# Delta net's values and keys turned by VectorE, second operands by operand for four output tiles, merges a step later

## The chip, the cores and the metric

The kernel runs on 1 core of one Trainium2 chip, in one launch. The metric is the device time of that core in microseconds (us), the median of three runs. The core has a matrix engine (PE), a vector engine (DVE), a scalar engine (ACT), GpSimd (POOL) and SyncE (SP), which here only issues DMAs; each works through its own instruction list in order and waits on semaphores.

## The reference

Two layers on a sequence of 1024 tokens and 1024 channels: layer 0 is a mixer of retention and a gated delta net, layer 1 a gated linear recurrence (RG-LRU); a feed-forward part with a causal convolution stands behind each, and every part begins with an RMS norm. The parts that the change touches are the delta net and the two output products `y @ w_out` and `(gelu(gate) * hs) @ lru_w_out`:

```python
qkv = jax.nn.silu(causal_dwconv(jnp.concatenate([q_d, k_d, v_d], axis=-1), conv_w))
...
lmat = jnp.where(strict, jnp.einsum('bhnid,bhnjd->bhnij', k_beta, kc) * decay, 0.0)
rhs = jnp.concatenate([vc * bc, k_beta * jnp.exp(gc)[..., None]], axis=-1)
sol = lax.linalg.triangular_solve(lmat + jnp.eye(c, dtype=jnp.float32), rhs,
                                  left_side=True, lower=True)
...
def step(s, inp):
    u_n, w_n, a_n, qd_n, kt_n, cd_n = inp
    v_new = u_n - jnp.einsum('bhcd,bhdv->bhcv', w_n, s)
    o = jnp.einsum('bhcd,bhdv->bhcv', qd_n, s) + jnp.einsum('bhij,bhjv->bhiv', a_n, v_new)
    s = s * cd_n + jnp.einsum('bhcd,bhcv->bhdv', kt_n, v_new)
    return s, o
...
y = jnp.concatenate([y_r, y_d.reshape(b, t, GDN_WIDTH)], axis=-1).astype(hn.dtype)
return y @ w_out
```

Four heads of 128 channels; the state is carried from chunk to chunk. Everything is float32.

## The kernel before

Activations lie in SBUF with channels on partitions and tokens along the row, in two halves of 512 tokens. A float32 product is made of three matmuls of rounded parts: `mm3` (L313 to L315) adds high times high, high times low and low times high. One such product of a 128x128 piece of a weight with 512 tokens is what the text calls a product, or a slot. P224, say, is the place in PE's list where 224 of them have run.

Weights arrive as "quarters" of 128x512 in an order fixed by a table. The SP queue loads one into a `raw` buffer (L257), ACT makes the rounded high part `whi` (L267), DVE subtracts to the low part `wlo` (L268). They are numbered from the kernel's start; six are held ready. Weights 44 and 45 are those of gate 14, weights 46 and 47 those of retention's q of head 0, 48 and 49 those of its k.

The order of each engine's list is set when the kernel is built, by a scheduler that takes the instructions as the program issues them and weighs when their operands come. The program issues side work in lanes, one step every two slots. In the delta net the lane runs, one after another: `subst`, a forward substitution of all 32x32 blocks on DVE (L1332, L1334), which stores the inverses to DRAM in two forms, `t_dram[0]` and `t_dram[1]` (L1337, L1339), then idles 11 steps; and a `merge` for each of four heads, which loads those blocks back, one form through SP and the other through POOL (L1353), and joins them to 128x128 inverses by small matmuls: L1369, L1378 and L1382, L1392, L1398 on PE, with copies between these on ACT (L1363, L1364, L1372, L1385, L1386, L1394, L1399) and L1400 on DVE. Beside this, the main stream projects units of 128 channels: q's heads, gates 12 and 13 (L1167 tanh on ACT, L1168 on DVE, stored to `g_dram`), v's heads, gate 14, then retention's q and k. A v head is evicted by L373, goes through its convolution (L1264 on ACT, L1266 three times on DVE) and an activation (L1268, L1269), and is stored to `v_dram` by one DMA of 512 KB (L1721). The rotary tables come by two DMAs that ACT issues (L1736 for the second) and are multiplied by the norm's row on DVE (L1737, L1738); retention's q and k are evicted with them (L1538, L1540, L1541).

The scan then runs over 8 chunks of 128 tokens. `scan_load` fetches v and q of a chunk (L1446, L1447). `scan_inside` turns v's four heads on PE with the identity (L1461) and scales the result out of PSUM on DVE (L1462), multiplies keys by queries (L1465), and turns K's four heads of the chunk (L1473, L1474) except in the last chunk. `scan_state` (L1485, L1491, L1498, L1508, L1509) carries the state.

`part` makes the two output products: for a group of output tiles m and each half u of the operands, it takes one quarter of tile m and multiplies it by its four operands in turn; in u == 1 the sum is added to the residual (L533). Groups are the first four output tiles of a half together, and then single tiles. The operands' rounded parts are made by L586 (ACT) and L587 (DVE).

Of the kernel before, what the change touches and what calls it, by code (L numbers as in the profile page):

```python
# [13 lines left out]
F32 = mybir.dt.float32  # L14
F32R = mybir.dt.float32r
AF = mybir.ActivationFunctionType
ALU = mybir.AluOpType
AX = mybir.AxisListType

P = 128  # L20
# [3 lines left out]
HALF = 512  # L24
NCH = T // P
NH = 4
# [72 lines left out]
def bc_last(ap, n):  # L99

    return ap.unsqueeze(2).to_broadcast([ap.shape[0], ap.shape[1], n])


class Block:
# [405 lines left out]
    def part(self, ys, name, groups, sl, each, kept=None):  # L510


        w = sl.stop - sl.start
        n, c0 = divmod(sl.start, HALF)
        for ms in groups:
            ps = {m: self.pp(both=True)[:, 0:w] for m in ms}
            for u in range(2):
                for m in ms:
                    if kept is None:
                        hi, lo = self.quarter((name + "ab"[u], m))  # L520
                    else:
                        if (u, m) not in kept:
                            kept[u, m] = self.load_kept(self.I[name + "ab"[u]][m], 4 * m + 2 * u)
                        hi, lo = kept[u, m]
                    nk = min(4, len(ys) - 4 * u)
                    for kt in range(nk):
                        c = slice(kt * P, (kt + 1) * P)
                        yh, yl = (a[:, c0:c0 + w] for a in ys[4 * u + kt][n])
                        self.mm3(ps[m], hi[:, c], lo[:, c], yh, yl, u == 0 and kt == 0, u == 1 and kt == nk - 1)
                        self.slot()  # L530
                    if u == 1:
                        h = self.H[m][:, sl]
                        self.nc.vector.tensor_tensor(h, ps[m], h, ALU.add)  # L533
                        each(m, h)
# [609 lines left out]
    def mix0(self, gain):  # L1144
        tc = self.tc
        self.q_dram = tc.dram_tile([NCH, P, HALF], F32, name="q_dram")
        self.ry_dram = tc.dram_tile([4, NCH, P, P], F32, name="ry_dram")
        self.v_dram = tc.dram_tile([NCH, P, HALF], F32, name="v_dram")
        self.gc_dram = tc.dram_tile([NH, NCH, P], F32, name="gc_dram")
        self.l_dram = tc.dram_tile([P, 32, 32], F32, name="l_dram")  # L1150
        self.t_dram = tc.dram_tile([2, P, 32, 32], F32, name="t_dram")
        self.y_dram = tc.dram_tile([8, P, T], F32, name="y_dram")
        self.rv_dram = tc.dram_tile([NCH, P, HALF], F32, name="rv_dram")
        self.g_dram = tc.dram_tile([NH, P, T], F32, name="g_dram")
        self.X = [[(self.slots1(4 * k + n), self.slots1(4 * k + 2 + n)) for n in range(2)] for k in range(KT)]
        with tc.tile_pool(name="l0", bufs=1) as pool:
            gd = self._mix0(pool.tile([P, 24 * HALF], F32, name="l0"))
        self.s2_stack = ExitStack()
        self.open_s2(self.s2_stack)
        self._mix0_out(gain, gd)  # L1160
# [10 lines left out]
    def _mix0(self, room):  # L1171
        tc, nc, I = self.tc, self.nc, self.I
        V, A, G, PE = nc.vector, nc.scalar, nc.gpsimd, nc.tensor
        H = self.H
        ps4 = lambda ps: ps.rearrange("p (h c) -> p h c", h=4)
        hs = lambda h: slice(h * P, (h + 1) * P)
# [83 lines left out]
        def conv_tail(kind, h, buf, dst):  # L1260
            ti = {"q": 0, "k": 4, "v": 8}[kind] + h
            c = self.t()
            w = lambda j: self.col("gdn_conv", 4 * ti + j)
            A.activation(c, buf[:, 1:1 + T], AF.Copy, scale=w(0))  # L1264
            for j in (1, 2, 3):
                V.scalar_tensor_tensor(c, buf[:, 1 + j:1 + j + T], w(j), c, ALU.mult, ALU.add)  # L1266
            th = self.t() if dst is None else dst
            A.activation(th, c, AF.Tanh, scale=0.5)  # L1268
            V.scalar_tensor_tensor(th, th, 1.0, c, ALU.add, ALU.mult)  # L1269
            return th  # L1270

        def conv_head(kind, h, dst):
            unit = conv_unit(kind, h)
# [169 lines left out]
        def scan_load(n):  # L1443
            t = chunk[n]
            t.update({"q": tmp2("qc"), "v": spare["v"][n % 2], "e": spare["e"][n % 2], "kt": spare["kt"][n % 2]})
            nc.sync.dma_start(t["v"], self.v_dram[n])  # L1446
            nc.sync.dma_start(t["q"], self.q_dram[n])  # L1447

        def scan_inside(n):
            cs = slice(n * P, (n + 1) * P)  # L1450
            cn = lambda t: hn(t)[:, :, n]
            q, v, gr, e, kt = (chunk[n][i] for i in ("q", "v", "gr", "e", "kt"))
            V.tensor_tensor(ps4(e), ps4(gr), bc_mid(sq["m_attn"], 4), ALU.add)
            for h in range(NH):
                A.activation(e[:, hs(h)], e[:, hs(h)], AF.Exp, bias=col(ngcc, h, n))
            for h in range(NH if n else 0):
                A.activation(gr[:, hs(h)], gr[:, hs(h)], AF.Exp, bias=col(cen, h, n))
            yield
            pv = self.pc()
            for h in range(NH):  # L1460
                PE.transpose(pv[:, hs(h)], v[:, hs(h)], self.ident)  # L1461
            V.tensor_tensor(ps4(v), ps4(pv), bc_last(cn(cv), P), ALU.mult)  # L1462
            p = self.pc()
            for h in range(NH):
                PE.matmul(p[:, hs(h)], K[h][:, cs], q[:, hs(h)], start=True, stop=True)  # L1465
            V.tensor_tensor(e, e, p, ALU.mult)
            if n:
                V.tensor_tensor(q, q, gr, ALU.mult)
            yield
            if n < NCH - 1:  # L1470
                p = self.pc()
                for h in range(NH):
                    PE.transpose(p[:, hs(h)], K[h][:, cs], self.ident)  # L1473
                V.tensor_tensor(ps4(kt), ps4(p), bc_last(cn(ekt), P), ALU.mult)  # L1474
            yield

        def scan_state(n):
# [213 lines left out]
        def subst():  # L1691
            yield from range(3)
            sub = subst_load()
            yield from range(2)
            for j in range(31):
                subst_step(*sub, j)
                yield
            subst_store(*sub)
            yield from range(11)
        gdn += [subst()]  # L1700
        for h in range(NH):
            gdn += [together(merge(h, 0), merge(h, 1))]
        for h in range(NH):
# [6 lines left out]
            if h % 2:  # L1710
                values(h // 2)

        def gates2(heads):
            for h in heads:
                g = self.gate2(self.unit("mix_in", 12 + h))
                nc.sync.dma_start(self.g_dram[h], g)
        scan_row(0)
        gates2((0, 1))
        for h in range(NH):
            v = conv_head("v", h, None)  # L1720
            nc.sync.dma_start(self.v_dram[:, :, hs(h)].rearrange("n p c -> p n c"),  # L1721
                              v.rearrange("p (n c) -> p n c", n=NCH))
        gates2((2,))
        self.flush()
        S = [tmp2("S0"), tmp2("S1")]
# [142 lines left out]
```

## Time and profile before

| | |
|---|---|
| median of 3 runs | 2149.26 us (2147.45 to 2149.64) |
| the profiled execution | 2149.09 us |
| its span, first to last instruction | 2147.3 us |
| mean granted clock of PE | 0.999 |
| moved by DMA | 307.98 MB, 143 GB/s over the span |

The profile's rows give line, engine, operation, output and input, with the count, and then busy time in us, mean in ns, and the idle time before with the instruction that ended it. Rows of a timeline begin with the start and the duration in us. Stretches of the delta net in the profiled execution: `subst` stores at 168.8 and 170.0 us, merges from 179.3 to 249, the scan's first chunk from 262.9, mix_out (layer 0's output product) around 490.

### The profile page before, as it was taken

Reading aid. Unit: us, or ns where it says so; the run is one execution under the profiler, and the core shown is the slowest. Engines: PE = TensorE matmul, PEld = TensorE weight load, DVE = VectorE, ACT = ScalarE, POOL = GpSimd, SP = SyncE. Lnnn points to the kernel's source line nnn. Section 1 sums busy time; section 2 is a strip of 40 time slices with the busy share of each in tenths; the row PEclk is TensorE's granted clock in tenths of the full one; section 3 lists DMA queues with packets and bytes.
Section 4 is the critical chain, followed back from the end, with each engine's and each line's share of the span. In section 5 each row is a group of like instructions: output and inputs, shape, how many; then the busy total and the mean of one; then the engine's idle time right before and its main releaser. Section 6 shows DMA issues by size and latency. Waiting matters only on the chain.

```text
span 2147.3 us, 29614 instructions
## 1 busy us (share of the span) xinstructions
PE 2131.8 (99%) x10652; PEld 1776.5 (83%) x10652; DVE 1704.7 (79%) x2581; ACT 1074.1 (50%) x1732; POOL 96.8 (5%) x114
## 2 busy tenths in 40 slices
PE   9999999999999999999999999999999999999998
PEld 7877888887888888888888888888888888888887
DVE  7995677766999989888766786778999889888645
ACT  6444522234665555555324476755655555554221
POOL 0102022200000000000000000000000000000001
PEclk9999999999999999999999999999999999999999
DMA  5354433543145435438725312252354445375542
GB/s 187 93 168 126 136 94 88 173 146 114 50 163 178 152 141 191 157 113 275 240 99 198 89 50 82 68 157 64 123 181 167 146 154 176 118 267 183 176 169 84
DMA packets 237171, 307.98 MB, mean 143 GB/s; under 512 B 62912, under 2 KB 125920, under 8 KB 237024
## 3 DMA queue, kind: packets, MB, share of 16 engines
q1 hardware_dynamic: 201344, 299.60, 41.8%
q10 hardware_dynamic: 34656, 5.97, 1.5%
q8 instruction: 84, 1.38, 0.3%
q0 software_dynamic: 1024, 0.53, 0.1%
q14 instruction: 63, 0.52, 0.1%
HBM read 215.27 MB, written 90.74 MB: 143 GB/s over the span
## 4 chain that ended last, share of the span: by engine, by line
PE 64%; issue 30%; DVE 3%; DMA 2%; POOL 0%; ACT 0%; SPq 0%; POOLq 0%; DVEq 0%; ACTq 0%
PE ps L313 19%; PE ps L315 19%; PE ps L314 19%; PE pc L313 1%; PE pc L314 1%; PE pc L315 1%; DVE h L973 0%; DVE l L1332 0%; DVE l L1334 0%; PE pc L1491 0%; PE pc L1577 0%; PE pc L1465 0%; PE ps L1509 0%; PE ps L1607 0%; DVE h L1303 0%
## 5 line engine op out<-in xcount | busy, mean ns | idle before, releaser
L313 PE MATMUL ps<-s,whi 128*128 128x512 f32 (+1 forms) x2704 | 1053.6, 390 | 2.5 <-ACT s L586 1.4
L314 PE MATMUL ps<-s,whi 128*128 128x512 f32 (+1 forms) x2704 | 1048.2, 388 | 1.2 <-DVE s L587 0.7
L315 PE MATMUL ps<-s,wlo 128*128 128x512 f32 (+1 forms) x2704 | 1047.5, 388 | 0.0
L267 ACT CAST whi<-raw 128x512 fp32r<-128x512 f32 (+1 forms) x620 | 377.0, 613 | 634.5 <-PE ps L314 499.7
L313 PEld LDWEIGHTS ps<-s,whi 128*128 128x128 f32 x2704 | 507.8, 188 | 108.2 <-ACT s L586 2.3
L314 PEld LDWEIGHTS ps<-s,whi 128*128 128x128 f32 x2704 | 508.0, 188 | 104.5 <-DVE s L900 1.8
L315 PEld LDWEIGHTS ps<-s,wlo 128*128 128x128 f32 x2704 | 507.7, 188 | 104.4 <-DVE wlo L268 0.6
L268 DVE TENSOR_TENSOR wlo<-raw,whi 128x512 fp32r<-128x512 f32 (+1 forms) x620 | 418.0, 680 | 64.0 <-ACT whi L267 55.2
L828 DVE SCALAR_TENSOR_TENSOR t<-halo,cols,t 128x1024 f32<-128x1024 f32 x176 | 221.7, 1281 | 2.1 <-ACT t L826 1.0
L801 DVE TENSOR_TENSOR halo<-ps,kept 128x512 f32<-128x512 f32 (+1 forms) x138 | 92.0, 667 | 76.4 <-PE ps L315 75.6
L811 DVE TENSOR_TENSOR h<-ps,h 128x512 f32<-128x512 f32 x112 | 77.3, 690 | 79.1 <-PE ps L315 79.1
L826 ACT ACTIVATE t<-halo,cols 128x1024 f32<-128x1024 f32 x88 | 109.6, 1247 | 18.0 <-DVE halo L801 9.9
L796 ACT COPY kept<-ps 128x512 f32<-128x512 f32 (+1 forms) x138 | 77.0, 558 | 11.0 <-PE ps L315 9.5
L533 DVE TENSOR_TENSOR h<-ps,h 128x512 f32<-128x512 f32 (+1 forms) x72 | 45.2, 630 | 42.0 <-PE ps L315 41.8
L916 DVE TENSOR_TENSOR t<-t 128x1024 f32<-128x1024 f32 x44 | 53.7, 1221 | 0.0
L911 ACT ACTIVATE t<-t 128x1024 f32<-128x1024 f32 x44 | 46.8, 1063 | 10.0 <-DVE t L828 10.0
L852 ACT CAST t<-t 128x512 fp32r<-128x512 f32 x56 | 34.0, 622 | 34.7 <-DVE t L916 32.7
L401 ACT ACTIVATE t<-h 128x512 f32<-128x512 f32 (+1 forms) x49 | 27.3, 563 | 44.2 <-DVE h L533 44.2
L313 PE MATMUL ps<-s,s 128*128 128x256 f32 (+1 forms) x144 | 46.0, 320 | 0.0
L314 PE MATMUL ps<-s,s 128*128 128x256 f32 (+1 forms) x144 | 45.8, 318 | 0.0
L315 PE MATMUL ps<-s,s 128*128 128x256 f32 (+1 forms) x144 | 45.8, 318 | 0.0
L1266 DVE SCALAR_TENSOR_TENSOR t<-halo,cols,t 128x1024 f32<-128x1024 f32 x33 | 41.9, 1278 | 2.9 <-ACT t L1264 2.6
(337 smaller groups left out, 2113.3 us busy)
## 6 DMA issues: line engine op xcount, KB each, us to landing
raw<-in_ffn_up_dram SPq DMA_DIRECT2D x176, 256.0 KB, 2.7
s<-pf_dram SPq DMA_DIRECT2D x112, 256.0 KB, 5.1
sf_dram<-t SPq DMA_DIRECT2D x72, 256.0 KB, 2.5
raw<-in_ffn_w_dram SPq DMA_DIRECT2D x64, 256.0 KB, 3.0
t<-sf_dram SPq DMA_DIRECT2D x58, 256.0 KB, 4.2
pf_dram<-t SPq DMA_DIRECT2D x56, 256.0 KB, 2.6
pf_dram<-lo SPq DMA_DIRECT2D x56, 256.0 KB, 2.6
raw<-in_mix_in_dram SPq DMA_DIRECT2D x52, 256.0 KB, 3.0
```

Source lines behind the costliest of these rows:

```text
L267: self.nc.scalar.copy(hi[:, 0:w], raw[:, 0:w])
L268: eng.tensor_tensor(lo[:, 0:w], raw[:, 0:w], f32(hi[:, 0:w]), ALU.subtract)
L313: mm(ps, whi, xhi, start=start, stop=False)
L314: mm(ps, whi, xlo, start=False, stop=False)
L315: mm(ps, wlo, xhi, start=False, stop=stop)
L796: A.copy(kept[o], ps)
L801: V.tensor_tensor(dst(i, j), v(ps), v(kept[k]), ALU.add)
L811: V.tensor_tensor(h(*to[o]), ps.rearrange("p (h c) -> p h c", c=256), h(*to[o]), ALU.add)
L826: A.activation(t, buf[:, 2:2 + T], AF.Identity, scale=w(0), bias=self.col(f"ffn_cb{layer}", tile_i))
L828: V.scalar_tensor_tensor(t, buf[:, 2 + j:2 + j + T], w(j), t, ALU.mult, ALU.add)
L911: A.activation(tg, tg, AF.Silu)
L916: V.tensor_tensor(tg, tg, tv, ALU.mult)
```

## The change

Three edits. In `part`, the second half of the operands of a group of four tiles takes its four quarters together and runs over the operands outside and the four tiles inside. In the delta net, DVE transposes each v head and each K head in blocks of 32x32 (one instruction for 128x1024), and four DMAs each, one for every 32 partitions, write the blocks turned to DRAM, in pieces of 32 numbers; a chunk's v and k are then loaded in the orientation that the scan needs, and PE's transposes go. `free[0]` is the buffer of the convolution that has become free; `slots(14 + ...)` are buffers that `subst` used. `subst` idles 12 steps instead of 11.

```diff
@@ part @@
             for u in range(2):
+                if u == 1 and len(ms) > 1:
+                    hold = self.qpos
+                    ws = [self.quarter((name + "b", m), 0, hold) for m in ms]
+                    for kt in range(len(ys) - 4):
+                        c = slice(kt * P, (kt + 1) * P)
+                        yh, yl = (a[:, c0:c0 + w] for a in ys[4 + kt][n])
+                        for m, (hi, lo) in zip(ms, ws):
+                            self.mm3(ps[m], hi[:, c], lo[:, c], yh, yl, False, kt == len(ys) - 5)
+                            self.slot()
+                    for m in ms:
+                        h = self.H[m][:, sl]
+                        self.nc.vector.tensor_tensor(h, ps[m], h, ALU.add)
+                        each(m, h)
+                    continue
...
@@ conv_head @@
             V.scalar_tensor_tensor(th, th, 1.0, c, ALU.add, ALU.mult)
+            free[0] = c
             return th
+
+        free = [None]
...
@@ scan_load @@
             nc.sync.dma_start(t["q"], self.q_dram[n])
+            if n < NCH - 1:
+                nc.sync.dma_start(t["kt"], self.k_dram[n])
...
@@ scan_inside @@
-            pv = self.pc()
-            for h in range(NH):
-                PE.transpose(pv[:, hs(h)], v[:, hs(h)], self.ident)
-            V.tensor_tensor(ps4(v), ps4(pv), bc_last(cn(cv), P), ALU.mult)
+            V.tensor_tensor(ps4(v), ps4(v), bc_last(cn(cv), P), ALU.mult)
...
-                p = self.pc()
-                for h in range(NH):
-                    PE.transpose(p[:, hs(h)], K[h][:, cs], self.ident)
-                V.tensor_tensor(ps4(kt), ps4(p), bc_last(cn(ekt), P), ALU.mult)
+                V.tensor_tensor(ps4(kt), ps4(kt), bc_last(cn(ekt), P), ALU.mult)
...
@@ subst @@
             subst_store(*sub)
-            yield from range(11)
+            yield from range(12)
...
+        def store_turned(dram, x, h, t):
+            V.transpose(t, x)
+            to = dram.rearrange("n (b i) c -> i (n b) c", i=32)
+            for d in range(4):
+                bs = slice(32 * d, 32 * d + 32)
+                nc.sync.dma_start(to[:, :, h * P + 32 * d:h * P + 32 * d + 32],
+                                  t[bs].rearrange("i (b j) -> i b j", j=32))
...
             v = conv_head("v", h, None)
-            nc.sync.dma_start(self.v_dram[:, :, hs(h)].rearrange("n p c -> p n c"),
-                              v.rearrange("p (n c) -> p n c", n=NCH))
+            store_turned(self.k_dram, K[h], h, slots(14 + 2 * (h % 2), 2))
+            store_turned(self.v_dram, v, h, free[0])
```

The scheduler orders the lists anew. Lines of the changed kernel are 14 to 22 higher behind `part`: L1387 there is L1369 here, L1396 and L1400 are L1378 and L1382, L1410 is L1392, L1416 is L1398, L1371 is L1353, L1182 and L1183 are L1167 and L1168, L1760 is L1738, L1552 to L1555 are L1538 to L1541.

The SP queue from the first store of `t_dram` on, before: loads of weights (`raw`, from `in_mix_in_dram`) stand between the merges' loads.

```order
L1337 DMA t_dram_111<-l0_118 128x1024
L1339 DMA t_dram_111<-l0_118 128x1024
L257 DMA raw_2091<-in_mix_in_dram 128x512
L1574 DMA l0_118<-rv_dram_113 128x4x128
L1353 DMA l0_118<-t_dram_111 32x4x32 x4
L1716 DMA g_dram_114<-t_1578 128x1024
L1353 DMA l0_118<-t_dram_111 32x4x32 x6
L257 DMA raw_2256<-in_mix_in_dram 128x512
L257 DMA raw_2262<-in_mix_in_dram 128x512
```

The same place now; `raw_2110` is weight 45, which was `raw_2091`, and `raw_2284` weight 46, which was `raw_2256`.

```order
L1355 DMA t_dram_112<-l0_119 128x1024
L1732 DMA k_dram_108<-l0_119 32x32x32
L1357 DMA t_dram_112<-l0_119 128x1024
L1732 DMA k_dram_108<-l0_119 32x32x32
L1738 DMA g_dram_115<-t_1579 128x1024
L1371 DMA l0_119<-t_dram_112 32x4x32 x8
...
L1732 DMA k_dram_108<-l0_119 32x32x32 x5
L1732 DMA v_dram_109<-t_1908 32x32x32 x4
L1732 DMA v_dram_109<-t_2086 32x32x32 x4
L257 DMA raw_2110<-in_mix_in_dram 128x512
...
L1732 DMA v_dram_109<-t_2266 32x32x32 x4
L257 DMA raw_2284<-in_mix_in_dram 128x512
```

(Repeated rows of the merges' loads and of k's stores between these are not shown.) Weight 45 now stands behind the stores of v's first two heads, weight 46 behind those of the third.

ACT's list before, where the cast of weight 46 (`whi_2258`) stands, in the middle of head 2's merge:

```order
L1386 ACTIVATE l0_118<-pc_2195 32x4x32
L267 CAST whi_2258<-raw_2256 128x512
L1394 COPY l0_118<-pc_2228 64x256
L1399 COPY h6_94<-l0_118 128x512
L1394 COPY l0_118<-pc_2234 64x256
```

And now (`whi_2286`), where `t_2557` is the tanh of gate 14:

```order
L1417 COPY h6_94<-l0_119 128x512
L1382 COPY l0_119<-l0_119 128x512 x2
L1758 DMA halo1_99<-in_rope_dram 128x1024
L1182 ACTIVATE t_2557<-t_2478 128x1024
L267 CAST whi_2286<-raw_2284 128x512
L267 CAST whi_2292<-raw_2290 128x512
```

DVE's list at that place, now; `ps_2531` is gate 14's second half, `ps_2614` the second half of retention's q of head 0:

```order
L373 TENSOR_TENSOR t_2478<-ps_2531,R_97 128x512
L1760 TENSOR_TENSOR halo1_99<-halo1_99,R_97 128x1024
L1183 SCALAR_TENSOR_TENSOR t_2478<-t_2557,t_2478 128x1024
L268 TENSOR_TENSOR wlo_2287<-raw_2284,whi_2286 128x512
...
L1552 TENSOR_TENSOR t_2580<-ps_2614,halo0_98 128x512
L1554 TENSOR_TENSOR l0_119<-ps_2614,halo1_99 64x512
L1555 TENSOR_TENSOR l0_119<-ps_2614,halo1_99 64x512
L268 TENSOR_TENSOR wlo_2469<-raw_2466,whi_2468 128x512
```

The cast and the low part of weight 46 moved behind gate 14's tanh and product, and the low part of weight 48 (`wlo_2469`) behind the evictions of the unit before it.

PE's list before, head 2's merge, of which the products between (L313 to L315) are left out; the rows stand four products apart:

```order
L1369 MATMUL pc_2134<-l0_118,h6_94 32x32 x8
L1369 MATMUL pc_2147<-l0_118,h6_94 32x32 x8
...
L1378 MATMUL pc_2172<-l0_118 32x32 x8
L1382 MATMUL pc_2173<-l0_118 32x32 x8
...
L1392 MATMUL pc_2228<-l0_118,h6_94 64x64 x4
```

The same merge now, without a row left out:

```order
L1387 MATMUL pc_2159<-l0_119,h6_94 32x32 x7
L314 MATMUL ps_2479<-s1_96,whi_2112 128x512
L315 MATMUL ps_2479<-s1_96,wlo_2113 128x512
L313 MATMUL ps_2479<-s1_96,whi_2112 128x512
L1387 MATMUL pc_2172<-l0_119,h6_94 32x32
L1396 MATMUL pc_2197<-l0_119 32x32 x8
L1400 MATMUL pc_2198<-l0_119 32x32 x8
```

It moved from P262 to P294, into gate 14 (`ps_2479`), and its links stand a product or less apart. Head 3's merge moved in the same way from P282 to P305.

More of the change, by code (lines that the diff above doesn't have):

```diff
@@ L1147, in mix0 @@
         self.ry_dram = tc.dram_tile([4, NCH, P, P], F32, name="ry_dram")
+        self.k_dram = tc.dram_tile([NCH, P, HALF], F32, name="k_dram")
         self.v_dram = tc.dram_tile([NCH, P, HALF], F32, name="v_dram")
```

## The prediction

> **What bounds the kernel now.** The page comes first, then TensorE's own waits.
>
> ```profile
> PE 2131.8 (99%) x10652; PEld 1776.5 (83%) x10652; DVE 1704.7 (79%) x2581; ACT 1074.1 (50%) x1732; POOL 96.8 (5%) x114
> ```
>
> ```profile
> PE ps L313 <- ACT s L586: 1.4, 2, 0.9
> ...
> PE pc L1369 <- DMA l<-t_dram: 1.0, 2, 0.6
> ...
> PE ps L314 <- DVE s L587: 0.7, 1, 0.7
> ```
>
> TensorE (PE) is busy for 99% of the span, and the waits shown, in us in total, times and the longest, are the three that the change touches. So an edit gains only what it takes out of PE's stream or waits, and loses whatever makes PE stand. I write P for the number of three-matmul products (L313 to L315) that PE has run; where two of them are one start to the next I use the cadence of these rows of PE's timeline (start, duration, idle before in brackets):
>
> ```profile
> 486.74 0.39 PE L314 MATMUL ps<-s,whi 128*128 128x512 f32 x1
> 486.97 0.39 PE L315 MATMUL ps<-s,wlo 128*128 128x512 f32 x1
> 488.26 0.50 PE L313 MATMUL ps<-s,whi 128*128 128x512 f32 x1 [0.90 <-ACT s L586]
> 489.42 0.50 PE L314 MATMUL ps<-s,whi 128*128 128x512 f32 x1 [0.66 <-DVE s L587]
> 491.81 0.50 PE L313 MATMUL ps<-s,whi 128*128 128x512 f32 x1 [0.52 <-ACT s L586]
> ```
>
> The first two start 0.23 us apart: a product costs 0.68 us, a duration of 0.39 notwithstanding.
>
> **Part 1, the transposes on PE.** Sixty go: 32 of v, 28 of K.
>
> ```profile
> L1473 PE MATMUL pc<-ident,h 128*128 128x128 f32 x28 | 4.2, 272 | 0.0
> L1461 PE MATMUL pc<-ident,l 128*128 128x128 f32 x16 | 2.4, 272 | 0.0
> L1461 PE MATMUL pc<-ident,kept 128*128 128x128 f32 x16 | 2.4, 272 | 0.0
> ```
>
> ```profile
> 262.63 0.39 PE L315 MATMUL ps<-s,wlo 128*128 128x512 f32 x1
> 262.86 0.60 PE L1461 MATMUL pc<-ident,kept 128*128 128x128 f32 x4
> 263.30 1.06 PE L1465 MATMUL pc<-l,h 128*128 128x128 f32 x8
> ...
> 265.58 0.60 PE L1473 MATMUL pc<-ident,h 128*128 128x128 f32 x4
> 265.94 0.48 PE L313 MATMUL ps<-s,whi 128*128 128x512 f32 x1
> ```
>
> The groups' busy time is 9.0 us, but neighbours overlap. From start to next start a group of four v transposes takes 0.44 us and a group of K 0.36 us, and the product behind a stand-alone group starts its second matmul about 0.1 us late. 8 x 0.44 + 7 x 0.36 + 7 x 0.1 = 6.7; some of the 0.1 stays where other small matmuls stand there, so I take **-6.5** (ends -6.1 and -9.0).
>
> [...]
>
> What replaces them: eight transposes of 128x1024 on VectorE (DVE) and 32 stores of 128 KB, each in 1024 pieces of 128 bytes, on the SP queue.
>
> ```profile
> L1426 DVE STREAM_TRANSPOSE l<-l 128x512 f32<-128x512 f32 x8 | 5.7, 708 | 0.1
> L1407 DVE STREAM_TRANSPOSE l<-pc 128x256 f32<-128x256 f32 x4 | 1.8, 438 | 0.0
> sum 120.00, PE 119.04 PEld 96.60 DVE 71.80 ACT 54.25 POOL 23.77; mean PE 19.84 PEld 16.10 DVE 11.97 ACT 9.04 POOL 3.96
> q10 hardware_dynamic: 34656, 5.97, 1.5%
> v_dram<-t SPq DMA_DIRECT2D x4, 512.0 KB, 4.1
> ```
>
> 256 more columns cost 0.27 us, so 1024 cost about 1.25 (an estimate) and eight 10 us. The third row sums the windows from 160 to 280 us: DVE is idle 48 of 120 us, which covers them; without that cover they would cost 10. The queue q10 moved 34656 packets, nearly all of 128 bytes, in 1.5% of 16 engines' span: 0.015 x 16 x 2147.3 / 34656 = 14.9 ns each. A store is then 1024 / 16 x 14.9 ns = 0.95 us of all engines, four of a head 3.8, against 4.1 to landing for the old v store. In bandwidth that is nothing; its ends are 0 and the rival below.
>
> **Part 2, mix_out.** The three gaps above are waits for second operands that arrive late; the starts show 0.90 + 0.66 + 0.52 = 2.1 us idle, and 488.26 - 486.97 - 0.23 = 1.06, 0.93 and 0.68 against the cadence: 2.7 us. With the operand loop outside, operand y2 is first wanted six products later than before and y3 nine, 4.1 and 6.1 us, more than any gap. **-2.7** (ends -2.1 and 0, if a held weight is late). In lru_out PE shows no wait on second operands, so 0.
>
> **Part 3, merges a step later.** A step is two products, 1.36 us, more than the old wait of 1.0 at L1369. But the order puts g_dram's store ahead of merge 0's loads on SP; that store waits for L1168 on DVE, which now stands behind the transpose of K1, which waits for t_dram[0] to land, at 174.05 as the first POOL load shows:
>
> ```profile
> L1353 POOL DMA_DIRECT2D l<-t_dram x32: 551/551/748, 174.0 to 223.5; - x32
> L1353 SPq DMA_DIRECT2D l<-t_dram x32: 303/382/967, 174.7 to 218.9; - x32
> ...
> DMA to landing us min/median/max: 1.6/2.3/4.6
> ```
>
> 174.05 + 1.25 + 0.69 + 1.23 = 177.2, the store's issue and eight loads of 0.38 to about 181, 2.1 to 2.3 to landing: 183.
>
> ```profile
> 179.28 0.44 PE L1369 MATMUL pc<-l,h 32*32 32x32 f32 x16
> ```
>
> PE wants the first two products later, at 180.6, and has about two products between the groups: some 1 to 2.4 us of waiting, taken at 2.0, where 1.0 was. **+1.0** (ends -1.0 and +2.5).
>
> **Part 4, what the order moves.** Merges 2 and 3 go from P262 and P282 to P294 and P305, and stand close; weights 45 to 49 load behind k's and v's stores. Rows for the steps:
>
> ```profile
> L1398 PE MATMUL pc<-l 64*64 64x64 f32 x64 | 4.6, 221 | 0.0
> L1372 ACT COPY l<-pc 32x128 f32<-32x128 f32 x16 | 4.1, 255 | 3.9 <-PE pc L1369 3.6
> L1264 ACT ACTIVATE t<-halo,cols 128x1024 f32<-128x1024 f32 x11 | 12.5, 1148 | 6.2 <-DVE halo L373 5.2 <-DVE l L1137 0.9
> L1266 DVE SCALAR_TENSOR_TENSOR t<-halo,cols,t 128x1024 f32<-128x1024 f32 x33 | 41.9, 1278 | 2.9 <-ACT t L1264 2.6
> halo<-in_rope_dram ACTq DMA_DIRECT2D x2, 512.0 KB, 4.0
> halo<-ry_dram SPq DMA_DIRECT2D x4, 512.0 KB, 5.7
> ```
>
> ```profile
> 223.45 0.62 ACT L267 CAST whi<-raw 128x512 fp32r<-128x512 f32 x1
> ...
> 255.92 1.06 ACT L1167 ACTIVATE t<-t 128x1024 f32<-128x1024 f32 x1
> ```
>
> ```profile
> 255.14 0.68 DVE L373 TENSOR_TENSOR t<-ps,R 128x512 f32<-128x512 f32 x1
> 255.74 0.68 DVE L268 TENSOR_TENSOR wlo<-raw,whi 128x512 fp32r<-128x512 f32 x1
> 257.01 1.23 DVE L1168 SCALAR_TENSOR_TENSOR t<-t 128x1024 f32<-128x1024 f32 x1 [0.59 <-ACT t L1167]
> 260.34 0.69 DVE L1538 TENSOR_TENSOR t<-ps,halo 128x512 f32<-128x512 f32 x1 [2.10 <-PE ps L315]
> ...
> 261.75 0.68 DVE L1541 TENSOR_TENSOR l<-ps,halo 64x512 f32<-64x512 f32 x1
> ```
>
> Merges 2 and 3: a merge gives ACT four copies of 0.26 (L1372), eight like them (L1385, L1386), two of L1394 (about 0.4, an estimate from these) and one whole buffer (0.62, as the cast below) between links: 4.5 us and, by the order, about 1 more of other work. PE has 3.6 us of products between the links of merge 2, 2.0 in merge 3, and its small matmuls, at most 4.6 / 4 = 1.15 us in each of five kinds. With full overlap PE waits near 0; with none it stands for about 3 in merge 2 and 4 in merge 3. The two halves overlap partly, and in merge 3 part falls into the next stall: **+1.5 and +2.0** (ends 0 and 7 together).
>
> P292: weight 45's low part, wlo, stands on DVE behind v3's first convolution step, which waits for ACT, which waits for the eviction after P288. 0.68 (eviction), 1.15 (L1264), 1.28 (L1266), 0.68 (wlo) and three handovers of 0.1 are 4.1, against four products and four matmuls that PE has meanwhile, 3.6. **+0.5** (0 to 2.5).
>
> P304: PE ends gate 14 and wants weight 46 at once. Before, its cast (223.45) stood far ahead of the gate's last eviction (255.14) and tanh (255.92). Now both are ahead of the cast: eviction 0.68, tanh 1.06, cast 0.62 and handovers: 2.6 us to the first matmul. Its third needs wlo, behind two DVE operations of 1.23, the rope product and L1168. The rope's transfer is issued by ACT only after both copies of merge 3's POOL loads, which wait for PE's merge 2, 7 us before P304. Four loads of 0.55 partly issued by then, 2.3 to landing and two copies of 0.62 put the issue 4.8 us into those 7, and 4.0 to landing ends at 8.9. Then 1.23 + 1.23 + 0.68: 12.0, so 5.0 after P304, in which PE runs two matmuls, 0.45. **+4.6** (ends 3.5, if the rope is in time, and 8.6, if a load and the rope take 4 us longer).
>
> P320: PE wants weight 48, and its wlo stands behind the three evictions of the product that PE has just ended, 260.34 to 262.43 before: 0.69 + 0.69 + 0.68 + 0.68 and 0.1, less two matmuls: **+2.4** (2.0 to 3.5). Before, DVE had idled 2.10 us ahead of those evictions with that wlo done.
>
> Later, chunk 5's state comes eight products later, and PE has products to run there: 0.
>
> The sum: -6.5 - 2.7 + 1.0 + 1.5 + 2.0 + 0.5 + 4.6 + 2.4 = **+2.8 us**. The profiled execution took 2149.09 (span 2147.3), the median 2149.26; 2.8 above them is 2151.9 and 2152.1. I forecast 2152.1.
>
> **Rivals.** *The waits are mostly covered*: ACT keeps up in both merges (0.3), merge 0's wait goes (-1.0), P292 costs 0, P304 3.5, P320 2.0. -6.5 - 2.7 - 1.0 + 0.3 + 3.5 + 2.0 = -4.4: 2144.9, and 2142.4 if the transposes give 9.0. For it: PE's waits in before are tiny with similar chains. Against: at P304 and P320 the order itself leaves PE nothing else.
>
> *The rope behind merge 3's copies*, slower: ACT issues the rope after copies that wait for POOL's loads. If these land at the row's maximum of 4.6 instead of 2.3, and the rope in 5.7, as ry_dram's loads of the same size, instead of 4.0, P304 costs 8.6, 4.0 more: 2156.1; the merges at 5.5, as the same copies are late, give 2158.1. It decides from the point where the rope lands more than 0.7 us after P304, since its product then ends after the tanh. Against: the median is 2.3.
>
> *Transposes by duration*: 60 x 272 ns = 16.3 us saved, 9.8 more: 2142.3. Against: the starts above.
>
> *The new stores are very slow*. If the pieces of a store went through one engine in place of 16, a head's four would take 4096 x 14.9 ns = 61 us.
>
> ```profile
> 250.79 0.37 SPq L1721 DMA_DIRECT2D v_dram<-t  x1
> ```
>
> The last v goes out near there and is wanted at 262.86, by the new order and the stalls some 15 us later: 250.8 + 61 - 277.9 = 34 us of standing, 2186. Against: queue q10's stores are cut as small, and four of them of 64 KB each are no late waits in this profile. [...]
>
> *The change doesn't do what it says in mix_out*: weights held by fours come late, the gaps return, 2154.8.
>
> **How the numbers follow.** About 0.2% (4.3 us) is what a measurement of this kernel can tell from no change: below 2145.0 is faster, above 2153.6 slower. Forecast (2148 to 2157) 0.42: same 0.27, slower 0.15. Covered waits 0.27: faster 0.18, same 0.09. Rope 0.16: slower. Duration 0.07: faster. Slow stores 0.03: slower. mix_out 0.05: same 0.02, slower 0.03. Faster 0.25, same 0.38, slower 0.37. The range reaches from 2141, the covered case with the transposes near 9, to 2160, the rope with P292 and merge 0 near their upper ends; the forecast alone is 2148 to 2157.
>
> **What would show it.** In the changed profile: PE's waits by ACT's cast and DVE's wlo near P304 and P320 (3.5 to 8.6 and 2.0 to 3.5 us), merges 2 and 3 close together with small waits, L1369 still waiting on t_dram, no wait for L586 or L587, a DVE transpose of about 1.25 us, and a store's landing under 5. PE at its full pace through P304 would prove me wrong, and so would a long wait for v or k at chunk 0.

## The result and the profile after

| | before | after |
|---|---|---|
| median | 2148.78 us (2147.45 to 2149.64, 4 runs) | 2164.52 us (2163.56 to 2165.96, 4 runs) |
| ratio, with its 95% interval | | 1.0074 (1.0062 to 1.0086) |
| span of the profiled execution | 2147.3 us | 2162.6 us |
| mean granted clock of PE | 0.999 | 0.994 |

The change makes the kernel slower by 0.74%, and the time lies above the predicted range. First the busy times on the page of the changed kernel, and the row of the granted clock in 40 slices of the span:

```profile
PE 2139.1 (99%) x10592; PEld 1778.5 (82%) x10592; DVE 1710.2 (79%) x2589; ACT 1071.4 (50%) x1732; POOL 98.2 (5%) x114
PEclk9999899999999999999999999999999999999999
```

PE runs 60 instructions fewer than before and is busy for 7.3 us longer. One slice, the fifth (216 to 270 us), has a lower clock. PE's waits in the changed kernel (total, times, the longest):

```profile
PE ps L315 <- DVE wlo L268: 2.9, 2, 2.5
PE pc L1505 <- DVE l L1501: 2.8, 1, 2.8
PE ps L313 <- ACT whi L267: 2.4, 1, 2.4
PE ps L1620 <- DVE l L1614: 2.2, 4, 1.0
...
PE pc L1387 <- DMA l<-t_dram: 0.8, 1, 0.8
```

The waits for L586 and L587 in mix_out are gone, and that for `t_dram` is 0.8 where it was 1.0. Four are new: weights at P304 and P320, and in the scan the product of a chunk's inverse with its corrected values (L1505, L1491 before) and retention's product with its own state (L1620). Now the stretch from P294 to P320 by windows: length, busy time and instructions of each engine, granted clock, DMA share, GB/s.

```profile
252.00:255.40 3.40, 1.02 (x4) 0.30 (x2) 2.96 (x4) 2.09 (x3) 0.00 (x0) 1.00 0.13 21
255.40:272.50 17.10, 16.72 (x149) 12.04 (x149) 2.12 (x5) 8.44 (x22) 0.00 (x0) 0.50 1.00 230
...
279.30:282.70 3.40, 1.03 (x4) 0.86 (x5) 3.31 (x5) 0.00 (x0) 1.73 (x1) 1.00 0.00 0
282.70:286.10 3.40, 3.40 (x10) 2.66 (x9) 3.40 (x6) 1.28 (x4) 0.06 (x1) 0.50 0.03 9
```

The first row is the stall at P304: PE works for 1.02 of 3.40 us. The second is the row that the prediction had no idea of: PE is busy, at a clock of 0.50, for 17.1 us. The last two are the same at P320, 3.4 us long. That is 20.5 us at half clock (17.1 + 3.4), so by estimate up to half of it, 10.2 us of time. The wider stretch of both kernels says it in two rows, after and then before:

```profile
238.00:286.00 48.00, 42.63 (x354) 30.95 (x353) 21.54 (x29) 19.56 (x50) 6.57 (x7) 0.79 0.61 135
```

```profile
220.00:262.00 42.00, 42.00 (x375) 33.68 (x374) 26.43 (x33) 23.37 (x56) 2.21 (x4) 1.00 0.46 142
```

Before, PE ran here without a gap and at the full clock. Now it is idle for 5.4 of 48 us and the mean clock is 0.79. PE's timeline shows both (start, duration, idle before and what ended it):

```profile
252.02 0.39 PE L315 MATMUL ps<-s,wlo 128*128 128x512 f32 x1
254.79 0.50 PE L313 MATMUL ps<-s,whi 128*128 128x512 f32 x1 [2.38 <-ACT whi L267]
...
256.14 0.79 PE L315 MATMUL ps<-s,wlo 128*128 128x512 f32 x1 [0.38 <-DVE wlo L268]
...
271.46 0.63 PE L314 MATMUL ps<-s,whi 128*128 128x512 f32 x1
271.88 0.63 PE L315 MATMUL ps<-s,wlo 128*128 128x512 f32 x1
272.85 0.40 PE L315 MATMUL ps<-s,wlo 128*128 128x512 f32 x1
...
281.67 0.50 PE L315 MATMUL ps<-s,wlo 128*128 128x512 f32 x1 [2.50 <-DVE wlo L268]
```

Near 271 a matmul takes 0.63 us and its neighbour starts 0.42 later; from 272.5 on 0.40 again, against the 0.39 and 0.23 shown before. The parts of the change itself came as they were meant. DVE's transposes in the groups, and the DMAs with their median to landing:

```profile
L1728 DVE STREAM_TRANSPOSE t<-t 128x1024 f32<-128x1024 f32 x4 | 5.0, 1246 | 0.1
```

```profile
k_dram<-l SPq DMA_DIRECT2D x16, 128.0 KB, 2.8
v_dram<-t SPq DMA_DIRECT2D x16, 128.0 KB, 3.4
kept<-v_dram SPq DMA_DIRECT2D x4, 256.0 KB, 6.1
kept<-k_dram SPq DMA_DIRECT2D x4, 256.0 KB, 5.7
```

A transpose of 128x1024 takes 1.25 us, a store of 1024 pieces lands in 2.8 to 3.4 us (medians). The loads of v and k shown, which are those of every other chunk, take about 6 us; those of the chunks between take 4.1 and 5.0. Before, v's took 3.9 and 3.0.

The profiled span grew by 15.3 us (2162.6 - 2147.3). The table says where it came from, after less before: PE's idle time, and for the rest the time from one start to the next, summed by group of instructions. The entries are rounded.

| | us |
|---|---|
| 60 transposes gone | -6.2 |
| idle in mix_out, merge 0 | -2.1, -0.2 |
| idle at P304 and P320 | +2.8, +2.5 |
| idle in the scan (L1505, L1620) | +5.4 |
| products L313 to L315, same number | +7.25 |
| the merges' small matmuls, same number | +4.0 |
| other small matmuls, idle elsewhere | about +2 |

### The profile page after: what moved, and what is told of

It is laid out like the page before. It is cut to its first block, busy times and chain, and to the rows that moved or that the text cites. A ratio compares the mean times of both kernels' runs of the same rounds, so it can differ in the third digit from the quotient of the medians.

```text
span 2162.6 us, 29544 instructions
## 1 busy us (share of the span) xinstructions
PE 2139.1 (99%) x10592; PEld 1778.5 (82%) x10592; DVE 1710.2 (79%) x2589; ACT 1071.4 (50%) x1732; POOL 98.2 (5%) x114
## 3 DMA queue, kind: packets, MB, share of 16 engines
q0 software_dynamic: 1024, 0.53, 0.1%
## 4 chain that ended last, share of the span: by engine, by line
PE 63%; issue 30%; DVE 4%; DMA 2%; POOL 1%; ACT 0%; SPq 0%; POOLq 0%; DVEq 0%; ACTq 0%
PE ps L313 19%; PE ps L315 19%; PE ps L314 19%; PE pc L313 1%; PE pc L314 1%; PE pc L315 1%; DVE wlo L268 0%; DVE h L987 0%; DVE l L1350 0%; DVE l L1352 0%; DMA l<-gc_dram 0%; PE pc L1505 0%; PE pc L1482 0%; DVE h L1321 0%; PE ps L1620 0%
## 5 line engine op out<-in xcount | busy, mean ns | idle before, releaser
L313 PE MATMUL ps<-s,whi 128*128 128x512 f32 (+1 forms) x2704 | 1054.5, 391 | 3.0 <-ACT whi L267 2.4
L315 PE MATMUL ps<-s,wlo 128*128 128x512 f32 (+1 forms) x2704 | 1050.5, 389 | 2.9 <-DVE wlo L268 2.9
L267 ACT CAST whi<-raw 128x512 fp32r<-128x512 f32 (+1 forms) x620 | 375.8, 612 | 609.5 <-PE ps L314 486.0
L313 PEld LDWEIGHTS ps<-s,whi 128*128 128x128 f32 x2704 | 509.1, 188 | 109.3 <-ACT whi L267 3.3
L315 PEld LDWEIGHTS ps<-s,wlo 128*128 128x128 f32 x2704 | 509.1, 188 | 108.0 <-DVE wlo L268 4.0
L268 DVE TENSOR_TENSOR wlo<-raw,whi 128x512 fp32r<-128x512 f32 (+1 forms) x620 | 416.1, 678 | 52.0 <-ACT whi L267 44.9
L547 DVE TENSOR_TENSOR h<-ps,h 128x512 f32<-128x512 f32 (+1 forms) x64 | 39.6, 620 | 33.1 <-PE ps L315 33.0
L313 PE MATMUL ps<-s,s 128*128 128x256 f32 (+1 forms) x144 | 46.0, 320 | 0.0
L315 PE MATMUL ps<-s,s 128*128 128x256 f32 (+1 forms) x144 | 45.8, 318 | 0.0
```

The source lines that it names most:

```text
L267: self.nc.scalar.copy(hi[:, 0:w], raw[:, 0:w])
L268: eng.tensor_tensor(lo[:, 0:w], raw[:, 0:w], f32(hi[:, 0:w]), ALU.subtract)
L313: mm(ps, whi, xhi, start=start, stop=False)
L315: mm(ps, wlo, xhi, start=False, stop=stop)
```

## The experiments

Two questions: which of the three edits costs the time, and whether the half clock or the waits themselves carry it. In each, "us" is the median, and the ratio is against the kernel before, run beside it.

**Splitting the change.** First only the turning, with `part` and the 11 idle steps as before:

```diff
-                if u == 1 and len(ms) > 1:
-                    ...
-            yield from range(12)
+            yield from range(11)
```

> Only the values and keys are turned by VectorE; the product loop of mix_out and the step of the merges are as in the kernel before. If the turning alone moves the merges and the weights (both theories say so), PE waits near P304 and P320 and the granted clock falls as in the changed kernel; without the 2.7 us of mix_out the time is 2166 to 2168. If instead the step of the merges or the operand loop had set off the loss, it is below 2150.

2165.99 us, ratio 1.0088 (1.0073 to 1.0103). Turning alone costs all of it. PE waits 2.4 us for a cast (L267) and 2.5 for a low part (L268), as in the changed kernel, and the mean granted clock of the profiled run is 0.994 in both. Then everything but the turning:

```diff
-            store_turned(self.k_dram, K[h], h, slots(14 + 2 * (h % 2), 2))
-            store_turned(self.v_dram, v, h, free[0])
+            nc.sync.dma_start(self.v_dram[:, :, hs(h)].rearrange("n p c -> p n c"),
+                              v.rearrange("p (n c) -> p n c", n=NCH))
```

The transposes run on PE as before.

> The kernel before with the operand loop and the later merges, without the turning. Expected: mix_out's three waits go (2.7 us) and merge 0's wait of 1.0 us goes or halves: 2145 to 2146.5, granted clock as before. If mix_out's gain was eaten by late weights: 2148 to 2149.

2145.45 us, ratio 0.9987 (0.9977 to 0.9996): 0.13% under the kernel before, less than the 0.2% that the prediction names as the limit, though the interval leaves 1 out. The longest of PE's waits in this kernel, which the kernel before has too, and one window at the place of P304:

```profile
PE pc L483 <- POOL rtok L466: 1.7, 2, 1.4
...
```

```profile
250.00:260.00 10.00, 10.00 (x46) 8.26 (x45) 7.42 (x11) 3.37 (x7) 0.00 (x0) 1.00 0.68 185
```

No wait of mix_out, of `t_dram` or for a weight is left, PE is busy for 10.00 of 10 us, and the clock is 1.00. Its two edits one by one, the operand loop alone (first) and the later merges alone:

> The kernel before with the operand loop of part alone. mix_out's three waits (2.1 us idle, 2.7 against the cadence) go and nothing else: 2145.0 to 2145.8, PE idle 2.1 us less than before, and L1369's wait of 1.0 us stays. If the gain of the run without turning came from the later merges instead: within 1 us of before.

> The kernel before with the merges a step later alone. L1369's wait of 1.0 us goes, as the loads are issued at the old times: 2146.7 to 2147.2. If the loads move with the merges, the wait stays and the time is that of before within 0.3 us.

2146.10 us, 0.9991 (0.9981 to 1.0000), and 2146.71 us, 0.9995 (0.9986 to 1.0004). Neither is told from 1 by itself, and the first is 0.3 us above what was expected of it. In the traces the waits for L586 and L587 are gone with the loop, and the wait for `t_dram` with the later merges. But these waits also vary between kernels that leave them alone: with the old loop PE waits for L586 and L587 2.1 us in the kernel before, 0.6 with the later merges alone and 0.5 with the turning alone; with the old merges it waits for `t_dram` 1.0 us before and 0.4 with the loop alone. One profile doesn't settle what either edit is worth.

**Filling the stalls.** Seven matmuls without use, on weights that are there, run at the head of the unit that stalls at P304:

```diff
+            for k in range(0 if n else busy):
+                self.nc.tensor.matmul(ps[0], self.hi[:, 0:P], self.X[k][0][0], start=True, stop=True)
...
-            self.project(unit, evac)
+            self.project(unit, evac, {0: 7, 4: 0}.get(ti, 0))
```

> The changed kernel with seven extra 128x512 matmuls on PE in the stall at P304 only, whose results are overwritten. Theory clock: the stall of 2.4 us in one window makes the clock fall to half for 17 us; with 1.6 us of the stall filled the clock stays at 1.0 there and the time falls by 8 to 9 us, to about 2156, with the waits of the other engines unchanged. Rival, packed merge: merge 3's chain is slow by itself and the low clock is only a sign of it: 2163 to 2166.

2163.78 us, ratio 1.0076 (1.0061 to 1.0091): a miss for the theory that the stall at P304 sets the clock. The windows of this kernel say why:

```profile
253.80:257.20 3.40, 2.15 (x9) 0.91 (x7) 3.30 (x4) 2.49 (x4) 0.00 (x0) 1.00 0.24 35
...
260.60:264.00 3.40, 3.11 (x59) 2.52 (x58) 0.22 (x1) 3.01 (x10) 0.00 (x0) 1.00 1.35 159
264.00:270.80 6.80, 6.80 (x23) 5.10 (x22) 0.61 (x2) 2.43 (x5) 0.00 (x0) 0.50 0.91 302
```

```profile
335.70:339.10 3.40, 0.63 (x5) 0.64 (x6) 3.32 (x8) 0.00 (x0) 0.99 (x1) 1.00 0.69 118
339.10:342.50 3.40, 3.40 (x13) 2.82 (x12) 0.82 (x2) 1.32 (x3) 0.28 (x1) 0.50 0.23 39
```

The window of the filled stall (PE busy 2.15 of 3.40) is followed by a clock of 1.00. But one in which PE is busy for 3.11 of 3.40, with merge 3's small matmuls (59 instructions), is followed by 6.8 us at 0.50; and the stall at L1505 (2.9 us) by 3.4 us at 0.50, as it is not in the changed kernel. So half clock came behind two things here: a stall, and a merge whose matmuls of 32x32 and 64x64 stand packed together. With eight more at P320 (`{0: 7, 4: 8}`):

> The same with eight more matmuls in the stall at P320. Theory clock: the second window of 3.4 us at half clock goes too, 1.7 us more: about 2154.5, and the granted clock is 1.0 up to the end of the kernel. Rival, packed merge: 2163 to 2166.

2161.44 us, ratio 1.0064 (1.0049 to 1.0079): between the two, so neither came true. Its four runs took 2158.39 and 2158.99 us at a mean granted clock of 0.998, and 2163.89 and 2164.11 at 0.995; the profiled one took 2158.99. In that one merge 3's window, as busy as the one above and with as many instructions, is followed by the full clock, and only 3.4 us at half clock are left, after the stall at L1505:

```profile
259.67:263.08 3.41, 3.12 (x59) 2.42 (x57) 0.00 (x0) 2.98 (x11) 0.00 (x0) 1.00 1.47 167
263.08:266.50 3.42, 3.42 (x21) 2.60 (x20) 0.83 (x2) 1.31 (x3) 0.00 (x0) 1.00 0.85 250
...
331.30:334.80 3.50, 0.69 (x4) 0.23 (x2) 3.42 (x7) 0.00 (x0) 0.17 (x1) 0.99 0.51 88
334.80:338.20 3.40, 3.22 (x12) 2.93 (x13) 1.64 (x5) 1.10 (x2) 1.09 (x1) 0.50 0.38 66
```

The fillers take the stalls' time (3.6 us of them, 3.3 us of waiting less), so the difference of the spans, 2162.6 - 2157.2 = 5.4 us, is by estimate about the price of the 17.1 us at half clock that went. The kernel's own four runs say the same: the same instructions take about 5 us longer where the granted clock is 0.995. So the clock counts, though for less than expected. The larger part is not the clock's: at a mean granted clock of 0.998, this run's span is still 9.9 us above that of the kernel before.

**Turning one of the two.** Only the keys turned by DVE, v stored whole and turned on PE; then only the values.

```diff
-            store_turned(self.v_dram, v, h, free[0])
+            nc.sync.dma_start(self.v_dram[:, :, hs(h)].rearrange("n p c -> p n c"),
+                              v.rearrange("p (n c) -> p n c", n=NCH))
```

> All three edits, but only the keys are turned by VectorE; the values go to DRAM whole and PE turns them. By the order merges 2 and 3 stand at P264 and P284 again with links four products apart, and weight 46 is cast well ahead of gate 14's tanh. Theory of the pile (late weights and packed merges make the stalls, and these the low clock): no stall over 1 us between 190 and 450 us, granted clock 1.0 there, and 2.7 to 3.3 us less than without turning: 2142 to 2143. Rival, small stores: sixteen stores in pieces of 128 bytes are slow by themselves: above 2146.

> All three edits, but only the values are turned. Merge 3 is packed at P306 to P309, weight 46 is cast ahead of the tanh. Theory of the pile: 3.5 us of transposes go, a packed merge costs 2 to 4: 2144 to 2147, with at most one window at half clock. Rival, small stores: as with the keys, above 2148.

2152.17 us, 1.0022 (1.0013 to 1.0032), and 2151.38 us, 1.0015 (1.0006 to 1.0024): both miss the theory, on the slow side, where the rival had them. With the keys alone the mean granted clock of the profiled run is 0.999, as in the kernel before, and most of PE's new waiting is in the scan. PE's waits there, and the DVE row behind the second (L1508 and L1491 are L1491 and L1474 of the kernel before):

```profile
PE pc L1508 <- DVE l L1504: 2.4, 4, 1.3
PE ps L1623 <- DVE l L1617: 2.1, 1, 2.1
```

```profile
300.43 0.69 DVE L1491 TENSOR_TENSOR l<-l 128x512 f32<-128x512 f32 x1 [3.21 <-DMA l<-k_dram]
```

DVE stands 3.2 us for a chunk of turned keys. Before, these came from SBUF through PE and waited for no DMA. With the values alone PE falls to half for one window, behind another packed merge 3 and no stall:

```profile
255.51 1.28 PE L1410 MATMUL pc<-l,h 64*64 64x64 f32 x16
...
257.08 0.68 PE L1416 MATMUL pc<-l 64*64 64x64 f32 x8 [0.29 <-ACT l L1412]
```

```profile
255.70:259.10 3.40, 3.11 (x35) 2.40 (x34) 0.41 (x1) 2.57 (x8) 0.00 (x0) 1.00 0.87 261
259.10:262.50 3.40, 3.40 (x9) 2.66 (x10) 0.42 (x1) 0.00 (x0) 0.00 (x0) 0.51 0.80 190
```

The keys once more, with the loads of k left out for chunks 2 to 6, so that they use what lies in the buffer:

```diff
-            if n < NCH - 1:
+            if n < 2:
                 nc.sync.dma_start(t["kt"], self.k_dram[n])
```

> As the run with the keys alone, but k's chunks 2 to 6 aren't loaded (the old contents are scaled in place). That run is 7 us above the one without turning in spite of a clock of 1.0. Theory loads: VectorE waits up to 3.2 us for a chunk of k ahead of what PE wants next, so without the loads the idle time of PE falls by 2 to 4 us and the time to 2147 to 2149. Rival, order: the scan's small matmuls are cut finer and stand badly whatever the loads do: 2151 to 2153.

2148.37 us, 1.0004 (0.9995 to 1.0014), 3.8 us under the keys alone. So the loads carry up to 3.8 of the 6.7 us by which the keys end above the kernel without turning (2152.17 - 2145.45), although 2.7 us of transposes are gone. In the profiles the 2.1 us at L1623 are gone with the loads; 1.0 us less is waited at merge 0, which these loads don't touch. The waits at L1508 stay at 2.1 us, without loads, so they do not hang on these loads.

**Moving the stores.** The k stores issued by the program behind all of v's, then all stores on ACT's queue, then weights 45 to 49 on ACT's queue:

```diff
             v = conv_head("v", h, None)
+            store_turned(self.v_dram, v, h, free[0])
+        for h in range(NH):
             store_turned(self.k_dram, K[h], h, slots(14 + 2 * (h % 2), 2))
-            store_turned(self.v_dram, v, h, free[0])
         gates2((2,))
```

> All of the change, but the four heads of K are turned and stored behind the last value. Merge 2 is at P264 with wide links, merge 3 packed at P307 to P310 behind the tanh. Theory of the pile: 6.2 us of transposes and 2.7 of mix_out go, merge 3 and one stall cost 3 to 8: 2142 to 2149. Rival, small stores: the 32 stores are the same, so 2160 or more.

2165.11 us, 1.0076 (1.0059 to 1.0093): a miss.

```profile
PE ps L313 <- ACT whi L267: 8.0, 1, 8.0
```

By SP's list the scheduler still puts six k stores early; ten stand together behind v's, the last of them for a transpose that DVE makes only at 272.3 us, and the loads of weights behind these. PE waits 8.0 us at P320. The clock is at half for about 6.8 and 10.2 us (worked out from 0.60, 0.72, 0.96, 0.50 and 0.52 in the windows of 5 us from 260 on), and for 3.4 in the scan (0.50 from 342.9).

```diff
-                nc.sync.dma_start(to[:, :, h * P + 32 * d:h * P + 32 * d + 32],
+                nc.scalar.dma_start(to[:, :, h * P + 32 * d:h * P + 32 * d + 32],
```

> All of the change, with the 32 stores issued by ScalarE's queue in place of SP's. The weights' loads on SP then stand behind no store; merge 2 ends at P283, merge 3 at P320. Theory of the pile: no stall near P304 and P320 from a weight, clock 1.0; 32 issues of 0.3 to 0.5 us on an engine that is half idle: 2138 to 2146. Rival, small stores: 2160 or more.

2172.01 us, 1.0111 (1.0096 to 1.0126): the worst. PE's waits of this kernel:

```profile
PE pc L1505 <- DVE l L1501: 6.3, 2, 5.5
PE ps L1620 <- DVE l L1614: 6.1, 5, 2.7
PE ps L313 <- ACT whi L267: 3.0, 1, 3.0
```

Off SP the stores no longer hold weight 46, and PE's wait at P304 is gone. The 3.0 us are at P320, for weight 48, whose cast stands in ACT's own list behind the issue of v's last four stores:

```profile
264.15 2.71 ACTq L1732 DMA_DIRECT2D v_dram<-t  x4
266.90 1.14 ACT L267 CAST whi<-raw 128x512 fp32r<-128x512 f32 x2 [5.32 <-DMA v_dram<-t]
```

In the scan PE waits 18.1 us in all, with the smaller rows, against 5.6 in the changed kernel, and the mean granted clock of the profiled run is 0.994. Why the scan waits so long here was not traced.

```diff
-                self.nc.sync.dma_start(raw[:, 0:w], src[:, c:c + w])
+                (self.nc.scalar if 45 <= seen < 50 else self.nc.sync).dma_start(raw[:, 0:w], src[:, c:c + w])
```

> The changed kernel with the loads of weights 45 to 49 issued by ScalarE's queue in place of SP's, so that none stands behind a store. By the order weights 46 and 48 are then cast long ahead of gate 14's tanh, merge 2 stays packed at P293 to P298, and merge 3 runs at P328 with no product between its links. Theory late weights: the waits at P304 and P320 (5.3 us) and the low clock that they set off go, and the time falls by 8 or more, to 2150 to 2156. Rival, packed merge: merge 3 without products between its links leaves PE to wait 4 us or more and to run small matmuls for a window or two, so waits and low clock come back near P328: 2160 to 2166.

2162.95 us, 1.0065 (1.0047 to 1.0083). PE's waits at P304 and P320 are gone and the time hardly moves, within the rival's range:

```profile
PE pc L1396 <- ACT l L1390: 2.2, 2, 1.9
```

```profile
270.00:280.00 10.00, 6.17 (x111) 5.55 (x110) 2.75 (x5) 6.08 (x17) 0.00 (x0) 0.56 0.20 60
280.00:290.00 10.00, 6.80 (x29) 5.97 (x28) 8.19 (x12) 4.22 (x14) 1.77 (x1) 0.50 0.65 207
```

Merge 3 now stands with no product between its links: PE waits for ACT's copies (L1390), is busy for 6.17 of 10 us with 111 instructions, most of them small, and the clock is at half for about 20.6 us, worked out from 0.56 and 0.50 here and 0.91 in the next 10 us. Merge 3's waits are only 2.2 us, though: the scan's first chunk, which now stands at the same place, waits for 4.9 us (L1482 for q 2.6, L1505 2.4), which the rival didn't count. Late weights are thus one form of the trouble, not its root.

## Why the prediction was wrong, by its steps

- **Transposes, -6.5:** measured -6.2. The count by starts, not by durations, was right; the rival of 16.3 falls, and with it its 2142.3.
- **mix_out, -2.7:** 2.1 us of idle are gone between the two profiles, and the edit alone gives 2146.10 against 2147.80 beside it, 1.7 us, with an interval that reaches 1. The kind is right. The size is not settled, since the old loop waits only 0.5 and 0.6 us in two other kernels.
- **Merge 0, +1.0:** -0.2. Waiting fell to 0.8 instead of growing to 2.0; in the three kernels with the later merges that turn no keys (without turning, later merges alone, values alone) it goes altogether. That fits the transpose of K1 holding back these loads ahead of L1168, for less than I had it.
- **P292, +0.5:** no wait there, its lower end.
- **P304, +4.6:** 2.8. The first wait, 2.38, is the 2.6 that the prediction worked out for ACT's cast. The second, 0.38 instead of 2.0, is small since the rope had landed. DVE's timeline:

```profile
252.44 0.69 DVE L373 TENSOR_TENSOR t<-ps,R 128x512 f32<-128x512 f32 x1 [2.58 <-PE ps L315]
253.05 1.22 DVE L1760 TENSOR_TENSOR halo<-halo,R 128x1024 f32<-128x1024 f32 x1
254.26 1.23 DVE L1183 SCALAR_TENSOR_TENSOR t<-t 128x1024 f32<-128x1024 f32 x1
```

  L1760 starts right behind the eviction and waits for no DMA. So the rope's rival falls.
- **P320, +2.4:** 2.5. Right.
- **Merges 2 and 3, +1.5 and +2.0:** the mechanism was wrong. PE hardly waits in them. It pays 4.0 us more for the same small matmuls. With both stalls filled, at a clock of 1.00 there, 2.2 of these stay, so by estimate about half is the clock's; that the rest is the packing's was not tested. With no stall just before it, a packed merge 3 was followed by half clock in three kernels (P304 filled, 0.50; k stores moved, 0.60 over 5 us; values alone, 0.51), and not in the profile with both stalls filled (1.00).
- **"Later, chunk 5's state comes eight products later, and PE has products to run there: 0":** wrong by 5.4 us. PE waits 2.83 and 0.4 us at L1505 and 2.2 at L1620. DVE's timeline, and then PE's:

```profile
336.79 0.69 DVE L1488 TENSOR_TENSOR kept<-kept,l 128x512 f32<-128x512 f32 x1 [2.91 <-DMA kept<-k_dram]
...
341.35 1.12 DVE L1501 SCALAR_TENSOR_TENSOR l<-pc,l 128x128 f32<-128x128 f32 x4
```

```profile
341.75 1.26 PE L1505 MATMUL pc<-l,h 128*128 128x128 f32 x8 [2.83 <-DVE l L1501]
```

  DVE, which makes that operand at L1501, stood itself 2.91 us for turned keys and had then no gap until L1501 (3.36 of 3.40 us busy in the window from 337.3). The run without loads shows that the loads are only a part of it. I had asked of the new loads only whether they are in time at chunk 0, which they were, and not whether a chunk's loads stay ahead through the scan.
- **The slow stores** (2186) fall: 2.8 to 3.4 us to landing, in pieces of 128 bytes. The milder rival of the experiments, that the stores cost time by themselves, is not settled: all four times that it named (above 2146 and 2148, twice 2160 or more) came true, and no run leaves the stores out and keeps the rest.

All that the prediction counted, transposes and waits, comes to -6.2 - 2.1 - 0.2 + 2.8 + 2.5 + 5.4 = +2.2 us, where it had +2.8. That is near by accident, since the merges and P304 were priced too high and the scan at nothing. The other 13 us are pace, not waits: 7.25 in the products, 4.0 in the merges, about 2 elsewhere. **Two steps failed. The first is that the sum priced a stall by its length alone.** It took PE's pace as given, 0.68 us a product, through stalls and packed merges. Right behind the stall of 2.4 us at P304 the clock was at 0.50 for 17.1 us, while PE ran the packed merge; behind the one of 2.5 us at P320, with products alone, for 3.4 us. That the merge kept it down is read from this difference and was not tested. By the profile with both stalls filled about 5.4 us hang on the clock, an estimate from the two spans; the products and the merges still take 2.2 us more each in it than in the kernel before. **The second is the scan, put at 0**, which cost 5.4 us of waits.

Neither the clock nor the waits are enough alone. Every kernel with both turned loses 13 to 24 us, whichever queue takes the stores; the forms differ: late weights, a packed merge 3, late keys in the scan. What they share is that 32 stores and eight more operations of DVE are put in among merges, weights and evictions. That the order which results is the common cause, leaving PE without products at one place or another, fits all of them and was not tested by itself.

Left open: why the scheduler places the weights and merge 3 as it does with the stores; what the half of the keys' loss is that stays without their loads (about 3 us over the kernel without turning, of which 2.1 are waits at L1508); and why the clock was lower in two of the four runs with both stalls filled, since no profile of these was taken.

## What to carry to other kernels

Price a new stall of PE by what stands behind it too, and look there at the granted clock: here stalls of 2.4 and 2.5 us were followed by 17.1 and 3.4 us at half clock. When work moves from a full engine to one with room, follow its operands through DRAM for every repetition of a loop, not only for the first, and count what else the moved instructions push together. Of a change in several parts, time each by itself: here a gain of 2.6 us (2148.0 to 2145.45) was hidden in a loss of 18 (to 2165.99).

## What the runs showed of the hardware

In the trace of the changed kernel the clock is at half from 255.4 us on for 17.07 us, then at full for 10.24 and at half again for 3.41: five, three and one times 3.41. In the other kernels the half clock read from the windows lasts about 3.4, 6.8, 10.2 and 20.6 us, near one, two, three and six times as long. The windows of 3.4 us shown here are counted from its changes.

Twice in the changed kernel half clock came right behind a window with PE busy for 0.30 of it (1.02 and 1.03 of 3.40), while the idle time at one stretch was only 2.4 and 2.5 us. A window with 0.48 was not followed by it:

```profile
337.30:340.70 3.40, 1.62 (x8) 1.00 (x6) 3.36 (x7) 0.00 (x0) 0.00 (x0) 1.00 0.36 66
340.70:344.10 3.40, 2.35 (x14) 2.14 (x15) 2.48 (x6) 1.05 (x2) 1.27 (x1) 1.00 0.57 97
```

Here lies the stall at L1505, as long (2.83 us) as the one of 2.9 that half clock followed with P304 filled: there it fell into one window (busy 0.63 of 3.40), here into two (1.62 and 2.35). So in this pair the length of the stall does not tell the two apart; the busy time of the window does. With both stalls filled and with the k stores moved the window at L1505 has PE busy for 0.69 of 3.50 and 0.70 of 3.40, and 0.50 follows in both. These are five windows with 0.19 to 0.30, all followed by half clock, and one with 0.48 that was not. Windows with a busier PE were followed by it too: those with 3.11 of 3.40 us, many of their matmuls small, were followed by 0.50 with P304 filled and by 0.51 with the values alone; with both stalls filled one with 3.12 of 3.41 was followed by 1.00. So the busy time alone does not order them all, and what does was not shown.
